# Second norm of a two-layer decoder: scale and shift as per-partition columns on the transposed blocks, on one Trainium2 core

## The chip, the cores and the metric

One core of a Trainium2 chip runs the whole program. The metric is the device time of one execution in microseconds (us), the median of several runs. The core has five engines with an instruction stream each: TensorE (PE, matrix products and transposes; its weight loads are shown apart as PEld), VectorE (DVE), ScalarE (ACT), GpSimdE (POOL) and SyncE (SP, which issues the DMAs). Each engine does its instructions in their order and waits on semaphores for the others.

## The reference

A token matrix x (1024 tokens, 1024 features, fp32) goes through two layers, each a mixer and a SwiGLU network. Each sub-layer normalises x, applies a shift and a scale that depend on a vector c, and adds its gated result to x:

```python
mod = (c_act @ ada_w[l] + ada_b[l])[:, None, :]
sh1, sc1, g1, sh2, sc2, g2 = jnp.split(mod, N_MOD, axis=-1)
...
x = x + g1 * (y @ w_out[l])
h = rms_norm(x, norm2_w[l]) * (1.0 + sc2) + sh2
gate, up = jnp.split(h @ w_gate_up[l], 2, axis=-1)
x = x + g2 * ((jax.nn.silu(gate) * up) @ w_down[l])
```

Here c_act is silu(c), and rms_norm(x, w) divides each token by the root of its mean square and multiplies feature by feature with w. The hidden width of the network is 2816. The change concerns the line that makes h: the scale (1 + sc2) times norm2_w, and the shift sh2, are 1024 numbers each, one a feature and the same for all tokens.

## The kernel before

**Tiles and precision.** The 1024 tokens lie as eight tiles X[t] of 128 tokens (partitions) by 1024 features. Products are done in fp32 accuracy by three matmuls of split operands (mm3, L134 to L136: high by high, high by low, low by high). A split (`split`) takes an ACT copy to the high half (L142) and a DVE subtraction for the low half (L139); hTh, hTl are the halves of the normalised input, gus those of the gate and up weights.

**Shift and scale.** The six modulation vectors of a layer come out of the products with ada_w as columns, mc, 128 partitions by 8 (feature 128 k + p stands in column k, partition p). ada_finish adds the bias (DVE, L380), for j = 4 forms (1 + sc2) times norm2_w (DVE, L383), turns the block on PE (L388, mcT), copies it from PSUM (ACT, L390, mr) and stores it to DRAM (L391). mod_row (L466) then reads a row back with a broadcast to all 128 partitions, 512 KB (L468, mrow). For the second norm that is j = 4 (scale) and j = 3 (shift), so that every partition holds the full row.

**The second norm.** norm2_a(t) calls rms_apply (L212): ACT squares the tile and sums along the row (L216, the square itself is thrown away into xn), POOL makes rs, the inverse root of the mean (ms and rs, L171 and L172), DVE computes x times rs times the scale row (L218, xn), and POOL adds the shift row (L220); for tile 3 DVE does this add. norm2_b(t) turns xn on PE, eight transposes of 128x128 (L478, hT, in two PSUM banks, kb = 0 and 1 for the lower and the upper four feature blocks), and ACT copies them out as hb, four copies of 128x256 a tile (L1386). In hb the features are on the partitions and the tokens along the row.

**The network.** Gate and up are computed by a Strassen-like scheme of seven products in the order b11, b21, t3, t2, t1, b22, t4. hb has four quarters: feature half kb by token half hf (hf 1 is tiles 4 to 7, hf 0 tiles 0 to 3). b11 and b21 are the two quarters of tiles 4 to 7, so they can start when those are normed; t3 and t2 are sums of quarters (build_t, whose additions are L1431, tile t), and t3, the first, needs quarters of tiles 0 to 3 too. That is why the norm's order is 4, 5, 6, 7, 0, 1, 2, 3: while the first products run, the last tiles are still normed, and behind tile 3 comes t3 = hb of tiles 0 to 3, upper features, less hb of tiles 0 to 3, lower features. The weights gur are loaded on SP's queue (L1439), combined on POOL (L1419) and split into gus. gu_pair adds products in the tiles p and u (p from gate by L1493 copies, L1498 additions from PSUM; silu on ACT, L1486, which has a table load ahead of it; the product, L1487; the store, L1488). The u copies are L1507 and L1512. Step functions run in an order given by strings of letters for each layer (O the output tile of the mixer, n and b the norm's two halves, h and t the splits); each also calls what it needs first. A scheduler then sets the order within each engine's stream from it, and pools of buffers (33 of 4 KB a partition in G, from which xn, hb and mrow are taken) limit what is under way. In the mixer's out_tile, DVE adds the group results oA, oB, oC of a tile to x (L1271) before the norm can take it.

Of the kernel before, what the change touches and what calls it, by code (L numbers as in the profile page):

```python
# [8 lines left out]
F32 = mybir.dt.float32  # L9
F32R = mybir.dt.float32r  # L10
I32 = mybir.dt.int32
AF = mybir.ActivationFunctionType
ALU = mybir.AluOpType
AX = mybir.AxisListType

P = 128
S = 1024
D = 1024
NT = S // P
KD = D // P  # L20
DEPTH = 2
# [25 lines left out]
R_N1, R_N2, R_AB, R_ON, R_BQ, R_BKV, R_BS, R_END = 0, 8, 16, 64, 72, 75, 77, 81  # L47
# [31 lines left out]
def tile_trunk(ctx, tc, x, c, positions, ada_w, ada_b, norm1_w, w_in, a_sinks, b_q_norm_w, b_w_uq,  # L79
# [3 lines left out]
    ACT, DVE, POOL, PE, DMA = nc.scalar, nc.vector, nc.gpsimd, nc.tensor, nc.sync  # L83

    cst = ctx.enter_context(tc.tile_pool(name="cst", bufs=1))
# [6 lines left out]
    def nm(s):  # L92
        uid[0] += 1
        return f"{s}_{uid[0]}"
# [13 lines left out]
    def G(shape, dt=F32, name="g"):  # L108
        return gp.tile(shape, dt, tag="g", name=nm(name), bufs=NG)
# [7 lines left out]
    def SM(shape, dt=F32, name="s"):  # L117
        return sp.tile(shape, dt, tag="s", name=nm(name))

    def TN(w=8, name="t"):  # L120
        t = tp.tile([P, 8], F32, tag="t", name=nm(name))
        return t[:, :w]

    def PA(name="pa"):
        return ps_pool["a"].tile([P, 512], F32, tag="a", name=nm(name))
# [43 lines left out]
    def rstd(dst, ss, n, w=1):  # L169
        v = TN(w, "ms")  # L170
        POOL.tensor_scalar(out=v, in0=ss, scalar1=1.0 / n, scalar2=EPS, op0=ALU.mult, op1=ALU.add)  # L171
        POOL.tensor_tensor(out=dst, in0=v, in1=mhalf[:, :w], op=ALU.pow)  # L172
# [39 lines left out]
    def rms_apply(xt, arow, shrow, eng=POOL):  # L212
        ss = TN(1, "ss")
        rs = TN(1, "rs")
        xn = G([P, D], F32, "xn")
        ACT.activation(out=xn, in_=xt, func=AF.Square, accum_out=ss)  # L216
        rstd(rs, ss, D)
        DVE.scalar_tensor_tensor(out=xn, in0=xt, scalar=rs, in1=arow, op0=ALU.mult, op1=ALU.mult)  # L218
        if shrow is not None:
            eng.tensor_tensor(out=xn, in0=xn, in1=shrow, op=ALU.add)  # L220
        return xn
# [76 lines left out]
    cols = []  # L298
# [66 lines left out]
    rows_done = set()  # L365
# [10 lines left out]
    cqd = [[dr.tile([P, 384], F32, name=f"cq{l}_{t}") for t in range(NT)] for l in range(DEPTH)]  # L376
    yad = [[dr.tile([P, 3, 512], F32, name=f"ya{l}_{hf}") for hf in range(2)] for l in range(DEPTH)]

    def ada_finish(l, j, mc, wait=1):
        DVE.tensor_tensor(out=mc, in0=mc, in1=cols[l][:, R_AB + 8 * j:R_AB + 8 * j + 8], op=ALU.add)  # L380
        if j in (1, 4):
            r = R_N1 if j == 1 else R_N2
            DVE.scalar_tensor_tensor(out=mc, in0=mc, scalar=1.0, in1=cols[l][:, r:r + 8],  # L383
                                     op0=ALU.add, op1=ALU.mult)
        for _ in range(wait):
            yield
        pt_ = PA("mcT")
        PE.transpose(pt_[:8, :P], mc, ident)  # L388
        mr = SM([P, 128], F32, "mr")
        ACT.copy(out=mr[:8, :], in_=pt_[:8, :P])  # L390
        DMA.dma_start(out=modd[l][j], in_=mr[:8, :])  # L391
        rows_done.add((l, j))
# [73 lines left out]
    def mod_row(l, j, alloc=G):  # L466
        t = alloc([P, D], F32, f"mrow{j}")
        DMA.dma_start(out=t, in_=modd[l][j].rearrange("r f -> (r f)").partition_broadcast(P))  # L468
        return t


    def transpose_tile(xn):

        r = []
        for kh in range(2):
            pv = PA("hT").rearrange("p (b f) -> p b f", f=P)
            for k in range(4):
                PE.transpose(pv[:, k, :], xn[:, (4 * kh + k) * P:(4 * kh + k + 1) * P], ident)  # L478
            r.append(pv)
        return r  # L480
# [66 lines left out]
    def layer(l, x_tiles):  # L547
# [32 lines left out]
        xns = {}  # L580
# [71 lines left out]
        if l == 0:  # L652
# [39 lines left out]
            def l_seq():  # L692
                for kp in range(4):
                    if kp >= 2:
                        need("a", 8)
                    raw_w.append(load_w1(kp, acc0[0]))
                    yield

            def s_seq():
                for kp in range(4):  # L700
                    need("l", kp + 1)
                    split_w1(raw_w[kp], POOL if SP0[kp] else DVE)
                    yield

            def h_seq():
                need("s", 2)
                for t in range(NE):
                    need("m", t + 1)
                    avq[t] = PA("avq")
                    in_proj(avq[t], T[t], w1, 0, 4)  # L710
                    yield

            def v_seq():
                need("s", 4)
                for t in range(NT):
                    if t < NE:
                        need("h", t + 1)
                    need("m", NE + t + 1 if t < NE else 2 * t + 2)
                    ps = avq[t] if t < NE else PA("avq")
                    in_proj(ps, T[t], w1, 4 if t < NE else 0)  # L720
                    avq_end(t, ps)
                    yield

            def c_seq():
                need("r", 2)
                consts.append(layer_consts(l, mod0[:, 4:5]))
                consts.append(setup_rest(mod0[:, 4:5]))
                run(consts[1])
                yield
                drain(consts[1])  # L730
                yield
# [5 lines left out]
            def bg_seq():  # L737
                need("C", 2)
                while run(bg):
                    yield  # L740

            def g_seq():
                need("r", 2)
                yield from g0
# [4 lines left out]
                                    l=l_seq(), s=s_seq(), h=h_seq(), v=v_seq(), C=c_seq(), G=g_seq(), B=bg_seq()))  # L749
# [483 lines left out]
        X = {}  # L1233
# [135 lines left out]
                yield  # L1369

        order = (4, 5, 6, 7, 0, 1, 2, 3)
        hb, hs, mods = {}, {}, []

        def norm2_a(t):
            xns[t] = rms_apply(X[t], mods[0], mods[1], DVE if t == 3 else POOL)
            DMA.dma_start(out=xm[l][t], in_=X[t])

        def norm2_b(t):
            hf, ts_ = t // 4, slice((t % 4) * P, (t % 4 + 1) * P)
            if t % 4 == 0:  # L1380
                for kb in range(2):
                    hb[kb, hf] = [(G if hf else W)([P, 2, 512], F32, "hb") for _ in range(2)]
            pvs = transpose_tile(xns.pop(t))
            for kb in range(2):
                for i in range(2):
                    ACT.copy(out=hb[kb, hf][i][:, :, ts_], in_=pvs[kb][:, 2 * i:2 * i + 2, :])  # L1386

# [232 lines left out]


        def mods_seq():
            mods.extend((mod_row(l, 4), mod_row(l, 3)))
            yield

        def norm_seq():
            need("k", 1)
            for n, t in enumerate(order):  # L1630
                need("O", 9 + n)
                norm2_a(t)
                yield

        def hb_seq():
            for n, t in enumerate(order):
                need("n", n + 1)
                norm2_b(t)
                yield
# [7 lines left out]
        def build_t_seq():  # L1647
            need("b", 8)
            need("h", 2)
            b11, b12, b21, b22 = hb[0, 1], hb[0, 0], hb[1, 1], hb[1, 0]  # L1650
            t2 = [G([P, 2, 512], F32, "t2") for _ in range(2)]
            tt2(t2, b22, b12, ALU.subtract)
            yield
            split_h("t3", t2)
            yield
            tt2(t2, t2, b11, ALU.add)
            split_h("t2", t2)
            yield
            tt2(b11, b12, b11, ALU.subtract)
            split_h("t1", b11)  # L1660
            yield
            split_h("b22", b22)
            yield
            tt2(b21, b21, t2, ALU.subtract)
            split_h("t4", b21)
            yield

        def load_gu_seq():
            gens[0] = gu_prep(load_gu(0))
            yield  # L1670

        def prep_gu_seq():
            need("j", 1)
            for n in range(2):
                ready.append(next(gens[0]))
                yield
# [12 lines left out]
        def pair_seq():  # L1689
            need("r", 2)  # L1690
            yield from pair_steps(0)

        seqs = dict(H=heads_seq(), S=soft_seq(), T=t_seq(), M=m_seq(), q=sq_seq(), a=ya_seq(), y=y_seq(), w=w_seq(),
                    g=g_seq(), x=x_seq(), O=o_seq(), k=mods_seq(), n=norm_seq(), b=hb_seq(), h=split_h_seq(),
                    t=build_t_seq(), j=load_gu_seq(), r=prep_gu_seq(), s=pair_seq())
        step, need = sequences(seqs)
# [34 lines left out]
        return X  # L1731

    X = layer(1, layer(0, None))
    fw = G([P, D], F32, "fw")
    DMA.dma_start(out=fw, in_=final_norm_w.partition_broadcast(P))
# [31 lines left out]
```

## Time and profile before

| what | value |
|---|---|
| median of the runs | 2379.6 us (2378.68 to 2386.13) |
| the profiled execution | 2386.33 us, of which 2384.6 us are the trace's span |
| mean granted clock of PE | 0.98 |
| DMA traffic | 349.78 MB, 147 GB/s over the span |
| stores to DRAM of modulation rows (L391) and broadcasts of them (L468) | 10 and 10 |
| shift additions on POOL / on DVE (L220) | 22 of 2.425 us mean / 2 of 1.22 us |
| copies hb (L1386) | 64 of 128x256, 0.388 us mean |

The profile is one execution. A row of a timeline has start, duration, engine, line, operation, the tiles written and read, and in brackets the time that the engine stood idle before it and what ended that idleness. A row of the waits has the waiting engine, tile and line, what it waited for, then the total, the number of times and the longest, in us. Of the 22 additions on POOL, 14 belong to the second norms and 8 to other norms; both on DVE belong to tile 3 of the second norms.

### The profile page before, as it was taken

The numbers are of one execution on the slowest core, as the hardware profiler recorded it, in microseconds if no ns is written. First come the engines' busy times: TensorE is split into PE (matmuls) and PEld (weight loads), VectorE is DVE, ScalarE is ACT, GpSimd is POOL, SyncE is SP. The second block draws the span as 40 slices with busy tenths as digits, with TensorE's granted clock in tenths as the row PEclk, the third lists the DMA queues.
The fourth block names the chain that finished last, engine by engine and source line by source line (L and its number), as shares of the span: only waits on it lengthen the run. The fifth ranks groups of instructions, "written<-read, shape, count | busy, mean of one in ns | idle before, by whom it ended". The sixth has DMA issues, their size and how long they took to land. (4 is left out here: it accounts for less than half of the span.)

```text
span 2384.6 us, 32002 instructions
## 1 busy us (share of the span) xinstructions
PE 2262.8 (95%) x11195; PEld 1907.2 (80%) x11195; DVE 1796.9 (75%) x2787; ACT 1099.1 (46%) x2244; POOL 1019.5 (43%) x1011
## 2 busy tenths in 40 slices
PE   5999899998999999999999899999989999999998
PEld 4789798887878787878878788988877888887786
DVE  7787578859768777699874875687698767648978
ACT  4566377625334343322344654784354444433233
POOL 4656630343323324455554655212435334225643
PEclk9999999999999999999999999999999999999999
DMA  7503432312566564872240154223125545467423
GB/s 254 165 19 113 170 131 89 112 48 93 168 208 233 178 235 167 307 274 89 80 162 22 55 178 142 80 80 115 54 84 188 192 154 181 164 219 288 155 106 115
DMA packets 156038, 349.78 MB, mean 147 GB/s; under 512 B 12619, under 2 KB 71781, under 8 KB 155877
## 3 DMA queue, kind: packets, MB, share of 16 engines
q1 hardware_dynamic: 155876, 347.74, 42.2%
q8 instruction: 88, 1.44, 0.2%
q14 instruction: 74, 0.60, 0.1%
HBM read 252.75 MB, written 94.94 MB: 146 GB/s over the span
## 5 line engine op out<-in xcount | busy, mean ns | idle before, releaser
L139 DVE TENSOR_TENSOR gus<-gur,gus 128x512 fp32r<-128x512 f32 x264 | 260.1, 1006 | 64.4 <-ACT gus L142 63.3
L142 ACT CAST gus<-gur 128x512 fp32r<-128x512 f32 x264 | 160.5, 621 | 223.9 <-PE gate L136 80.3
L134 PE MATMUL gate<-hTh,gus 128*128 128x512 f32 x616 | 243.3, 395 | 11.9 <-ACT u L1507 11.9
L134 PE MATMUL down<-dnt,dns 128*128 128x512 f32 x616 | 241.8, 393 | 11.6 <-issue 6.3
L135 PE MATMUL gate<-hTl,gus 128*128 128x512 f32 x616 | 241.8, 393 | 4.4 <-DVE hTl L139 4.4
L134 PE MATMUL up<-hTh,gus 128*128 128x512 f32 x616 | 241.8, 393 | 3.8 <-ACT u L1512 3.6
L135 PE MATMUL down<-dnt,dns 128*128 128x512 f32 x616 | 241.0, 391 | 1.3 <-DVE dnt L139 1.3
L136 PE MATMUL gate<-hTh,gus 128*128 128x512 f32 x616 | 241.5, 392 | 0.0
L135 PE MATMUL up<-hTl,gus 128*128 128x512 f32 x616 | 240.9, 391 | 0.0
L136 PE MATMUL down<-dnt,dns 128*128 128x512 f32 x616 | 240.9, 391 | 0.0
L136 PE MATMUL up<-hTh,gus 128*128 128x512 f32 x616 | 240.5, 390 | 0.0
L1419 POOL TENSOR_TENSOR gur<-gur 128x512 f32<-128x512 f32 x44 | 64.5, 1465 | 393.7 <-DVE gus L139 364.4
L142 ACT CAST dns<-act 128x512 fp32r<-128x512 f32 x132 | 81.8, 622 | 248.9 <-PE down L136 190.0
L1597 DVE TENSOR_TENSOR x<-x,down 128x512 f32<-128x512 f32 x224 | 147.9, 678 | 29.2 <-PE down L136 28.9
L139 DVE TENSOR_TENSOR dns<-act,dns 128x512 fp32r<-128x512 f32 x132 | 137.7, 1057 | 14.3 <-ACT dns L142 14.2
L134 PEld LDWEIGHTS gate<-hTh,gus 128*128 128x128 f32 x616 | 116.5, 189 | 39.6 <-ACT u L1507 14.9
L134 PEld LDWEIGHTS down<-dnt,dns 128*128 128x128 f32 x616 | 116.4, 189 | 39.1 <-issue 7.4
L135 PEld LDWEIGHTS gate<-hTl,gus 128*128 128x128 f32 x616 | 116.7, 189 | 29.7 <-DVE hTl L139 6.0
L134 PEld LDWEIGHTS up<-hTh,gus 128*128 128x128 f32 x616 | 116.6, 189 | 29.1 <-ACT u L1512 4.5
L135 PEld LDWEIGHTS down<-dnt,dns 128*128 128x128 f32 x616 | 116.4, 189 | 25.7 <-DVE dnt L139 1.7
L136 PEld LDWEIGHTS up<-hTh,gus 128*128 128x128 f32 x616 | 116.5, 189 | 24.6
L136 PEld LDWEIGHTS gate<-hTh,gus 128*128 128x128 f32 x616 | 116.5, 189 | 24.5
(410 smaller groups left out, 6158.8 us busy)
## 6 DMA issues: line engine op xcount, KB each, us to landing
gur<-in_w_gate_up_dram SPq DMA_DIRECT2D x88, 512.0 KB
ada<-in_ada_w_dram SPq DMA_DIRECT2D x80, 512.0 KB
wp<-wpe SPq DMA_DIRECT2D x77, 512.0 KB
dnt<-wp SPq DMA_DIRECT2D x77, 512.0 KB
dnr<-in_w_down_dram SPq DMA_DIRECT2D x44, 512.0 KB
act<-act SPq DMA_DIRECT2D x44, 512.0 KB
wr<-in_w_in_dram SPq DMA_DIRECT2D x24, 512.0 KB
act<-u SPq DMA_DIRECT2D x44, 256.0 KB
```

What stands on the lines that cost most here:

```text
L134: PE.matmul(ps, lh, rh, start=start, stop=False, skip_group_check=more)
L135: PE.matmul(ps, lh, rl, start=False, stop=False, skip_group_check=more)
L136: PE.matmul(ps, ll, rh, start=False, stop=stop, skip_group_check=more)
L139: eng.tensor_tensor(out=out_, in0=a, in1=b, op=ALU.subtract)
L142: ACT.copy(out=h, in_=src)
L1419: return lambda o, a, b, op: eng.tensor_tensor(out=o, in0=a, in1=b, op=op)
L1597: DVE.tensor_tensor(out=av_, in0=av_, in1=ps[t], op=ALU.add)
```

## The change

The columns of shift and scale stay where they are made. A constant tile modc[l], 128 by 16, holds the shift in columns 0 to 7 and the scale in columns 8 to 15, and ada_finish writes them there with the DVE steps that it had; for j = 3 and 4 it returns then, so the transpose, copy and store are gone, and so are the two broadcasts in mods_seq. norm2_a keeps the square and the inverse root; DVE multiplies x by rs alone (a tensor_scalar), and nothing is added. norm2_b applies scale and shift when it takes a transposed block out of PSUM: feature block k has its scale and shift in one column of modc, so ACT does eight activations a tile (Identity with a scale and a bias column, 128x128 each) instead of four copies. Four of tile 3, kb = 1, are DVE's (tensor_scalar, multiply and add).

```diff
+    modc = [cst.tile([P, 16], F32, name=f"modc{l}") for l in range(DEPTH)]
     def ada_finish(l, j, mc, wait=1):
-        DVE.tensor_tensor(out=mc, in0=mc, in1=cols[l][:, R_AB + 8 * j:R_AB + 8 * j + 8], op=ALU.add)
+        d = modc[l][:, 8 * (j == 4):8 * (j == 4) + 8] if j in (3, 4) else mc
+        DVE.tensor_tensor(out=d, in0=mc, in1=cols[l][:, R_AB + 8 * j:R_AB + 8 * j + 8], op=ALU.add)
         if j in (1, 4):
             r = R_N1 if j == 1 else R_N2
-            DVE.scalar_tensor_tensor(out=mc, in0=mc, scalar=1.0, in1=cols[l][:, r:r + 8],
+            DVE.scalar_tensor_tensor(out=d, in0=d, scalar=1.0, in1=cols[l][:, r:r + 8],
                                      op0=ALU.add, op1=ALU.mult)
+        if j in (3, 4):
+            rows_done.add((l, j))
+            return
...
         def norm2_a(t):
-            xns[t] = rms_apply(X[t], mods[0], mods[1], DVE if t == 3 else POOL)
+            ss = TN(1, "ss")
+            rs = TN(1, "rs")
+            xn = xns[t] = G([P, D], F32, "xn")
+            ACT.activation(out=xn, in_=X[t], func=AF.Square, accum_out=ss)
+            rstd(rs, ss, D)
+            DVE.tensor_scalar(out=xn, in0=X[t], scalar1=rs, scalar2=None, op0=ALU.mult)
...
         def norm2_b(t):
...
-            pvs = transpose_tile(xns.pop(t))
-            for kb in range(2):
-                for i in range(2):
-                    ACT.copy(out=hb[kb, hf][i][:, :, ts_], in_=pvs[kb][:, 2 * i:2 * i + 2, :])
+            for kb, pv in enumerate(transpose_tile(xns.pop(t))):
+                for i in range(4):
+                    d, k = hb[kb, hf][i // 2][:, i % 2, ts_], 4 * kb + i
+                    a, b = modc[l][:, 8 + k:9 + k], modc[l][:, k:k + 1]
+                    if t == 3 and kb == 1:
+                        DVE.tensor_scalar(out=d, in0=pv[:, i, :], scalar1=a, scalar2=b, op0=ALU.mult, op1=ALU.add)
+                    else:
+                        ACT.activation(out=d, in_=pv[:, i, :], func=AF.Identity, scale=a, bias=b)
...
         def mods_seq():
-            mods.extend((mod_row(l, 4), mod_row(l, 3)))
+            assert {(l, 3), (l, 4)} <= rows_done
```

The change also moves instructions, alike in both layers. Names carry a number for each buffer; line numbers in the new kernel are 16 higher behind the norm. The next rows are DVE's stream in layer 1 from the scaling of tile 3 (xn) to the low half of the first t3 operand (hTl), as it was:

```order
L218 SCALAR_TENSOR_TENSOR xn_16942<-x_16441,rs_16941,mrow_3257_16407 128x1024
L139 TENSOR_TENSOR gus_17051<-gur_16665,gus_17051 128x512
L220 TENSOR_TENSOR xn_16942<-xn_16942,mrow_3258_16409 128x1024
L1498 TENSOR_TENSOR p_3344_16829<-p_3344_16829,gate_16888 128x512
L139 TENSOR_TENSOR gus_17054<-gur_16669,gus_17054 128x512
L139 TENSOR_TENSOR gus_17059<-gur_16667,gus_17059 128x512
L1431 TENSOR_TENSOR t_3366_16964<-hb_16799,hb_16797 128x1024
L1431 TENSOR_TENSOR t_3367_16965<-hb_16800,hb_16798 128x1024
L1498 TENSOR_TENSOR p_3344_16829<-p_3344_16829,up_16889 128x512
L1487 TENSOR_TENSOR p_3344_16829<-p_3344_16829 128x512
L139 TENSOR_TENSOR hTl_16969<-t_3366_16964,hTh_16968 128x1024
```

And as it is in the changed kernel:

```order
L1386 TENSOR_SCALAR xn_16961<-x_16439,rs_16960 128x1024
L139 TENSOR_TENSOR gus_17073<-gur_16667,gus_17073 128x512
L139 TENSOR_TENSOR gus_17076<-gur_16671,gus_17076 128x512
L1514 TENSOR_TENSOR p_3332_16841<-p_3332_16841,gate_16900 128x512
L139 TENSOR_TENSOR gus_17081<-gur_16669,gus_17081 128x512
L1400 TENSOR_SCALAR hb_16807<-hT_16973,modc_357 128x128 x2
L1400 TENSOR_SCALAR hb_16808<-hT_16973,modc_357 128x128 x2
L1514 TENSOR_TENSOR p_3332_16841<-p_3332_16841,up_16901 128x512
L1447 TENSOR_TENSOR t_3354_16986<-hb_16807,hb_16805 128x1024
L1447 TENSOR_TENSOR t_3355_16987<-hb_16808,hb_16806 128x1024
L1503 TENSOR_TENSOR p_3332_16841<-p_3332_16841 128x512
L139 TENSOR_TENSOR hTl_16991<-t_3354_16986,hTh_16990 128x1024
```

The shift's addition is gone, four evictions (hb) have come, and the addition of the up product to p, which needs PE's last matmul of it, stands ahead of the two t steps instead of behind them.

POOL's stream in layer 1 from tile 1's to tile 3's inverse root, before:

```order
L171 TENSOR_SCALAR ms_16791<-ss_16787 128x1
L172 TENSOR_TENSOR rs_16788<-ms_16791,mhalf 128x1
L220 TENSOR_TENSOR xn_16789<-xn_16789,mrow_3258_16409 128x1024
L1419 TENSOR_TENSOR gur_16667<-gur_16667,s_3313_16731 128x4x128
L171 TENSOR_SCALAR ms_16906<-ss_16902 128x1
L172 TENSOR_TENSOR rs_16903<-ms_16906,mhalf 128x1
L220 TENSOR_TENSOR xn_16904<-xn_16904,mrow_3258_16409 128x1024
L1419 TENSOR_TENSOR gur_16671<-gur_16671,s_3314_16732 128x4x128
L171 TENSOR_SCALAR ms_16944<-ss_16940 128x1
L172 TENSOR_TENSOR rs_16941<-ms_16944,mhalf 128x1
```

And now:

```order
L171 TENSOR_SCALAR ms_16800<-ss_16796 128x1
L172 TENSOR_TENSOR rs_16797<-ms_16800,mhalf 128x1
L1435 TENSOR_TENSOR gur_16669<-gur_16669,s_3301_16741 128x4x128
L1435 TENSOR_TENSOR gur_16673<-gur_16673,s_3302_16742 128x4x128
L171 TENSOR_SCALAR ms_16918<-ss_16914 128x1
L172 TENSOR_TENSOR rs_16915<-ms_16918,mhalf 128x1
L171 TENSOR_SCALAR ms_16963<-ss_16959 128x1
L172 TENSOR_TENSOR rs_16960<-ms_16963,mhalf 128x1
```

The additions are gone, and both weight combinations (gur) now stand ahead of the inverse root of tile 2 (the second ms and rs), where one stood ahead and one behind.

More of the change, by code (lines that the diff above doesn't have):

```diff
@@ L1371, in layer @@
         order = (4, 5, 6, 7, 0, 1, 2, 3)
-        hb, hs, mods = {}, {}, []
+        hb, hs = {}, {}
         def norm2_a(t):
-            xns[t] = rms_apply(X[t], mods[0], mods[1], DVE if t == 3 else POOL)
+            ss = TN(1, "ss")
[4 more added lines that the diff above has]
+            DVE.tensor_scalar(out=xn, in0=X[t], scalar1=rs, scalar2=None, op0=ALU.mult)
             DMA.dma_start(out=xm[l][t], in_=X[t])
```

## The prediction

> **What bounds the kernel now.** I read the engine totals first, then TensorE's waits, then the timelines round the longest of those that the change can reach.
>
> ```profile
> PE 2262.8 (95%) x11195; PEld 1907.2 (80%) x11195; DVE 1796.9 (75%) x2787; ACT 1099.1 (46%) x2244; POOL 1019.5 (43%) x1011
> ...
> PE gate L134 <- ACT u L1507: 11.9, 6, 2.8
> PE hT L478 <- DVE xn L220: 9.9, 2, 5.0
> PE hT L478 <- POOL xn L220: 6.5, 3, 4.1
> ...
> PE gate L135 <- DVE hTl L139: 4.4, 2, 2.2
> ```
>
> PE is busy 95% of the span, so an edit to other engines pays only where PE stands still. It stands still for the second norm in three rows (total, times, longest): twice 5.0 us, once a layer, for the shift added to token tile 3 (L220, on DVE); for POOL's adds (1.2 us in each second norm; the third, 4.1, is a first norm, untouched); twice 2.2 us for the first low half made behind it (hTl). That is some 8.4 us a layer. PE there, in layer 1 (start, duration, idle before and releaser), the same place in layer 0 (555.13), and layer 1's stretch with its granted clock, 0.77:
>
> ```profile
> 1710.94 1.09 PE L478 MATMUL hT<-ident,xn 128*128 128x128 f32 x8 [1.23 <-POOL xn L220]
> ...
> 1738.72 1.97 PE L478 MATMUL hT<-ident,xn 128*128 128x128 f32 x8 [4.95 <-DVE xn L220]
> ...
> 1741.34 0.63 PE L136 MATMUL up<-hTh,gus 128*128 128x512 f32 x1
> 1741.77 0.63 PE L134 MATMUL up<-hTh,gus 128*128 128x512 f32 x1
> ...
> 1744.49 0.39 PE L136 MATMUL up<-hTh,gus 128*128 128x512 f32 x1
> 1744.72 0.40 PE L134 MATMUL gate<-hTh,gus 128*128 128x512 f32 x1
> ...
> 1747.59 0.50 PE L135 MATMUL gate<-hTl,gus 128*128 128x512 f32 x1 [2.24 <-DVE hTl L139]
> ...
> 555.13 1.97 PE L478 MATMUL hT<-ident,xn 128*128 128x128 f32 x8 [4.95 <-DVE xn L220]
> ...
> 1730.00:1745.00 15.00, 10.05 (x47) 8.42 (x46) 12.47 (x15) 9.02 (x21) 4.73 (x4) 0.77 0.31 105
> ```
>
> Behind the 4.95 us stall the matmuls take 0.63 instead of 0.39 us (a step of 0.43, where 1744.49 to 1744.72 has 0.23). Eight transposes and twelve matmuls last from 1738.72 to 1744.88, 6.2 us; at full clock about 0.85 for the transposes (1.09 with its overlap, 1710.94) and 12 x 0.23 = 2.8, 3.6 in all. So the stall costs some 2.5 us more. Layer 0 stalls as long, at 555.13.
>
> **The change part by part.** I follow layer 1; DVE first.
>
> ```profile
> 1720.52 4.18 DVE L139 TENSOR_TENSOR hTl<-hb,hTh 128x1024 fp32r<-128x1024 f32 x2
> ...
> 1727.61 1.29 DVE L218 SCALAR_TENSOR_TENSOR xn<-x,rs,mrow 128x1024 f32<-128x1024 f32 x1 [1.65 <-POOL rs L172]
> 1728.81 0.69 DVE L139 TENSOR_TENSOR gus<-gur,gus 128x512 fp32r<-128x512 f32 x1
> ...
> 1730.08 2.23 DVE L139 TENSOR_TENSOR gus<-gur,gus 128x512 fp32r<-128x512 f32 x1
> 1732.23 0.74 DVE L1271 SCALAR_TENSOR_TENSOR x<-oB,rsb,x 128x512 f32<-128x512 f32 x1
> ...
> 1735.64 1.28 DVE L218 SCALAR_TENSOR_TENSOR xn<-x,rs,mrow 128x1024 f32<-128x1024 f32 x1 [0.44 <-POOL rs L172]
> ...
> 1737.44 1.22 DVE L220 TENSOR_TENSOR xn<-xn,mrow 128x1024 f32<-128x1024 f32 x1
> ...
> 1741.13 2.36 DVE L1431 TENSOR_TENSOR t<-hb,hb 128x1024 f32<-128x1024 f32 x2 [0.67 <-ACT hb L1386]
> ...
> 1744.91 0.69 DVE L1498 TENSOR_TENSOR p<-p,up 128x512 f32<-128x512 f32 x1 [1.42 <-PE up L136]
> ...
> 1746.32 2.35 DVE L139 TENSOR_TENSOR hTl<-t,hTh 128x1024 fp32r<-128x1024 f32 x2
> ```
> ```profile
> 1720.08 2.40 POOL L220 TENSOR_TENSOR xn<-xn,mrow 128x1024 f32<-128x1024 f32 x1 [1.59 <-DVE xn L218]
> 1725.38 1.28 POOL L1419 TENSOR_TENSOR gur<-gur,s 128x512 f32<-128x512 f32 x1 [2.90 <-DVE gus L139]
> ...
> 1729.04 2.72 POOL L220 TENSOR_TENSOR xn<-xn,mrow 128x1024 f32<-128x1024 f32 x1 [1.47 <-DVE xn L218]
> ...
> 1734.73 0.88 POOL L172 TENSOR_TENSOR rs<-ms,mhalf 128x1 f32<-128x1 f32 x1
> ```
> ```profile
> 1733.00 1.06 ACT L216 ACTIVATE xn<-x 128x1024 f32<-128x1024 f32 x1 [5.42 <-DVE x L1271]
> ...
> 1735.56 2.28 ACT L1386 COPY hb<-hT 128x256 f32<-128x256 f32 x8
> ...
> 1741.39 1.28 ACT L1486 ACT_TABLE_LOAD   x1
> 1742.68 0.63 ACT L1486 ACTIVATE p<-p 128x512 f32<-128x512 f32 x1
> 1743.22 1.03 ACT L142 CAST hTh<-t 128x1024 fp32r<-128x1024 f32 x1
> ```
>
> *POOL's adds go.* While one runs, DVE is slow beside it: the hTl pair takes 4.18 us under the add of 1720.08 and 2.35 without one; a gus takes 2.23 under the add of 1729.04 and 0.69 without. That is 1.83 and 1.54 us.
>
> *The scaling loses its second tensor.* The xn step (1.28) becomes x times rs. The trace has an operation of DVE with one tensor source of this size:
>
> ```profile
> L254 DVE TENSOR_SCALAR acc<-ada,cact x10: 735/746/1847, 94.3 to 1403.7; 128x1024 f32<-128x1024 f32 x10
> 264.93 0.37 ACT L834 ACTIVATE QK<-ukv,rskv 128x128 f32<-128x128 f32 x1 [0.53 <-PE ukv L136]
> 265.20 0.46 ACT L836 ACTIVATE QK<-ukv,rskv 128x256 f32<-128x256 f32 x1
> ```
>
> I take its median, 0.75, so 0.5 us less each time.
>
> *Up to tile 3's sum.* rs of tile 2 now stands behind both of POOL's gur steps (one moves ahead, 1.28). They start at 1725.38 − 1.83 = 1723.55, end at 1726.1, and rs follows at 1726.9; xn ends at 1727.65 instead of 1728.8. One gus has moved ahead of it, so oA's sum (0.75), a gus (0.69) and oB's sum (0.74) end at 1729.8, where now it is 1732.97: 3.2 us earlier. Bounds: 0, if POOL's rs comes as late as DVE saves, and 4.4, if rs has no wait at all (1.65 less, short of what the moved gus takes).
>
> *Tile 3.* From the square's start to xn's it is 1735.64 − 1733.00 = 2.64; so xn runs from 1732.4 to 1733.2, and the shift's 1.22 us with the gus ahead of it is gone (1738.7 now). PE, rid of tile 7's wait of 1.23, is free for tile 3 at 1738.72 − 4.95 − 1.23 = 1732.5: a stall of 0.7 instead of 4.95, and up ends 3.6 us later, at 1736.8 instead of 1744.9.
>
> *ACT is next in line.* Eight and four copies of 128x256 before the table load become sixteen and four activations of 128x128, each with a scale and a bias column. They begin where the copies began, shifted by the square: 1735.56 − 3.2 = 1732.4. Their price isn't in the trace. The nearest rows: an activation of 128x128 from PSUM with one column takes 0.37 and lets the next one start after 0.27; copies step 2.28/8 = 0.285. The upper end is 0.46, the full duration of the row of twice the size. I take 0.36, about the full duration of the one-column row, nearest to it in size and operands. Then 20 x 0.36 = 7.2 us, to 1739.6; at 0.27, 1.8 us sooner; at 0.46, 2.0 later.
>
> The Trainium skill, page "ScalarE: Activation LUTs", section "What ACT_TABLE_LOAD costs", gives an activation 186 ns + 0.833 ns an element, about 93 ns more for each column operand and about 93 ns of overlap with the next. For the one-column row that is 386 ns, near the 0.37 here; for two columns it would be a step of 0.386, 20 of them 7.7 us, and the sum 1.0 us worse over both layers.
>
> *Then DVE.* The two t (1.18 each) run 1739.6 to 1742.0; the product p (0.69) waits for the table (1.28) and silu, 1741.5, so it ends at 1742.7. The cast on ACT ends at 1742.5. From hTl's start to PE's it is 1747.59 − 1746.32 = 1.27: PE resumes at 1744.0, **3.6 us earlier**. The add p<-p,up, moved ahead of t, costs nothing: up is done at 1736.8, 3 us before t can start. The four evictions that DVE takes (one-tensor operations) lie beside ACT's.
>
> *What comes back.* PE now idles from 1736.8 to 1744.0, more than 4.95, so the slow clock comes after it: 2.5 us over the next products. Behind them PE waits again, for a chain that starts with DVE behind this tile and goes through POOL and a load, so it moves up by the 3.6:
>
> ```profile
> 1765.23 1.82 DVE gus L139 x3
> ...
> 1799.14 0.50 PE L134 MATMUL gate<-hTh,gus 128*128 128x512 f32 x1 [2.52 <-ACT u L1507]
> ...
> 613.73 0.50 PE L134 MATMUL gate<-hTh,gus 128*128 128x512 f32 x1 [1.09 <-ACT u L1507]
> ...
> 327.93 0.27 PE L388 MATMUL mcT<-ident,mc 128*8 128x128 f32 x1 [1.24 <-DVE mc L380]
> ```
>
> The 2.52 cover the 2.5 in layer 1. In layer 0 the same wait is 1.09 (613.73), and 1.4 us are lost.
>
> *At nothing.* Per layer two mcT transposes, two small copies and stores, and two broadcasts of a row to 512 KB leave. The only one of the removed transposes that PE waited for cost 1.24 us (327.93, for DVE mc); other work of PE may take its place: 0, bounds 0 to 1.2 in all. The broadcasts land long before they are used: 0, bounds 0 to 1.0. They leave SP's queue; a gur load in layer 1 goes ahead of a store and three loads, inside the DMA time of the chain above: 0.
>
> *Sum.* 2 x 3.6 − 1.4 = 5.8 us. The profiled execution is 2386.3 (its span 2384.6), 6.7 over the median of 2379.6; both lose as much: 2380.5, and **2373.8 for the median**. About 0.3%, 7.1 us (2372.5 to 2386.7 counts as the same), is what can be told from no change.
>
> **The rivals.**
> *Cheap evictions.* ACT steps 0.27 as behind the one-column row, so 1.8 a layer more: 5.4 x 2 − 1.4 = 9.4, 2370.2; with 4.4 upstream instead of 3.2, 2367.8. For it: copies step 0.285. Against it: a second column.
> *The slow clock decides.* If PE has no wait left behind the gap that takes the slow clock in, 2.5 is lost in both layers: 2 x (3.6 − 2.5) = 2.2, 2377.4. For it: 0.63 us matmuls after 4.95 us of idleness, and the gap here is 7.2; and the wait of 2.52 ends with a load, not with DVE. The Trainium skill, page "TensorE: Matmul & The Clock Gate", section "What's actually happening", has half rate after an idle window of about 3.4 us until one such window is busy; the 0.77 agrees. By it the gap makes PE slow in both layers for some 3.4 us, a loss of about 1.7 each, an estimate; this rival would then give 2 x 1.9, 2375.8.
> *Dear evictions.* At 0.46, 2.0 a layer less: 1.6 x 2 − 1.4 = 1.8, 2377.8; with half of the 3.2 upstream, 2381.0.
> *Slower: the add ahead of t.* p<-p,up waits for PE's up matmuls, and now the two t and all behind them on DVE queue behind it. If tile 3's xn comes no earlier than now, up ends at 1744.9 as now; then 0.7 + 2.36 + 0.69 and the 1.27 give 1749.9, 2.3 a layer later, and a second slow clock (2.5) may follow: 2 x 2.3 to 2 x 4.8, 2384 to 2389, 2386 likeliest. It costs from where tile 3's transposes start behind 1736.4 (6.2 to up's end and 5.0 behind it make 1747.6). For it: a wait of DVE on PE in the row of 1744.91. Against it: 3.2 us upstream, and the shift's 1.22.
>
> **How the numbers follow.** Forecast 0.44 (its own range 2370.5 to 2377; faster 0.18, same 0.26). Cheap evictions 0.20, faster. Slow clock 0.14, same. Dear evictions 0.10, same. Add ahead of t 0.12 (slower 0.10, same 0.02). So faster 0.38, same 0.52, slower 0.10. The range goes from 2367 (cheap, with early upstream, and 0.8 of the removed waits) to 2381 (dear, late upstream); outside are the slower rival and a little.
>
> **What would show it.** Right: the wait hT <- DVE xn falls to under 1.5 us in each layer; no 2 us gus round tile 2's norm; activations of hb at a step near 0.36; a PE gap of 6 to 8 us before the first t3 product with matmuls of 0.63 behind it. Wrong: a step of 0.27 or 0.46; t waiting for p<-p,up; a hT wait that stays near 5; hTl pairs that remain above 4 us (then DVE was not slowed by POOL).

## The result, and the profile after

The changed kernel takes 2371.5 us (median of 14 runs, 2367.0 to 2378.6) where the kernel before takes 2385.3 (14 runs, 2378.7 to 2389.3): ratio 0.9948, 95% interval 0.9940 to 0.9957. By the ratio that is 12.4 us less, by the medians 13.8, where the prediction had 5.8. The forecast of 2373.8 lies close, and the range holds the time, but the closeness is luck: the forecast started from the first three runs of before, whose median of 2379.6 turned out 5.7 us low, and that hid most of a gain that was put too small. Measured as a difference, the gain is twice the forecast.

The engine totals and TensorE's waits of the changed kernel (total, times, longest; its line numbers are 6 to 16 higher):

```profile
PE 2258.4 (95%) x11191; PEld 1904.2 (80%) x11191; DVE 1775.4 (75%) x2793; ACT 1120.9 (47%) x2296; POOL 984.8 (42%) x997
...
PE gate L134 <- ACT hTh L142: 8.1, 2, 4.1
PE gate L134 <- ACT u L1523: 6.9, 6, 1.8
...
PE hT L484 <- POOL xn L220: 4.1, 1, 4.1
...
PE hT L484 <- DVE p L1514: 2.3, 2, 1.1
...
PE hT L484 <- DVE xn L1386: 0.4, 2, 0.2
```

The two stalls of 4.95 us for tile 3 are 0.2 us each, tile 7's 1.2 us are gone, and so are the 2.2 us for hTl. In their place PE waits 4.1 us a layer for the first cast of t3 (hTh), and 1.1 us for DVE's addition p<-p,gate, which frees the PSUM bank of tile 3's second half. That wait stood nowhere in before: there the transposes began so late (1738.72) that this addition ended (1739.26) while the first half was being turned.

The same place in layer 1 on PE, DVE and ACT. All of it lies 11.2 us earlier than in before already when the stretch begins:

```profile
1721.26 0.66 PE L484 MATMUL hT<-ident,xn 128*128 128x128 f32 x4 [0.21 <-DVE xn L1386]
1723.06 0.66 PE L484 MATMUL hT<-ident,xn 128*128 128x128 f32 x4 [1.14 <-DVE p L1514]
...
1730.54 0.79 PE L134 MATMUL gate<-hTh,gus 128*128 128x512 f32 x1 [4.05 <-ACT hTh L142]
...
1731.80 0.79 PE L135 MATMUL gate<-hTl,gus 128*128 128x512 f32 x1
1732.39 0.63 PE L136 MATMUL gate<-hTh,gus 128*128 128x512 f32 x1
```
```profile
1709.49 1.23 DVE L139 TENSOR_TENSOR hTl<-hb,hTh 128x1024 fp32r<-128x1024 f32 x1 [1.06 <-ACT hTh L142]
...
1715.26 0.75 DVE L1386 TENSOR_SCALAR xn<-x,rs 128x1024 f32<-128x1024 f32 x1 [2.68 <-POOL rs L172]
...
1716.59 0.68 DVE L139 TENSOR_TENSOR gus<-gur,gus 128x512 fp32r<-128x512 f32 x1
1717.19 0.74 DVE L1277 SCALAR_TENSOR_TENSOR x<-oB,rsb,x 128x512 f32<-128x512 f32 x1
...
1726.53 0.69 DVE L1514 TENSOR_TENSOR p<-p,up 128x512 f32<-128x512 f32 x1 [1.41 <-PE up L136]
1727.13 2.35 DVE L1447 TENSOR_TENSOR t<-hb,hb 128x1024 f32<-128x1024 f32 x2
```
```profile
1720.53 7.08 ACT L1402 ACTIVATE hb<-hT,modc 128x128 f32<-128x128 f32 x20
1727.63 1.28 ACT L1502 ACT_TABLE_LOAD   x1
```

The hTl step takes 1.23 and the gus 0.68 us, where before had 4.18 for a pair and 2.23. The twenty activations take 7.08 us, a step of 0.354. Then the slow clock (0.63 us matmuls, the granted clock at half) comes behind the gap.

To see where the 15.8 us between the two profiled spans (2384.6, 2368.8) arise, each PE matmul of one trace is set beside the same matmul of the other. The table gives the time from one place of the program to the next in us, the places named by before's time there, for every kernel of this study, one profile each:

| kernel | to 300 | 300–345 | 515–650 (norm 0) | 650–960 | 960–1690 | 1690–1815 (norm 1) | 1815–2375 |
|---|---|---|---|---|---|---|---|
| before | 300.0 | 45.0 | 135.0 | 310.0 | 730.0 | 125.0 | 560.0 |
| before, again | 301.5 | 45.0 | 135.4 | 306.8 | 734.5 | 123.7 | 563.3 |
| changed | 299.3 | 44.1 | 131.7 | 304.5 | 729.2 | 120.3 | 560.1 |
| changed, again | 299.4 | 44.1 | 131.4 | 302.8 | 730.9 | 119.7 | 558.8 |
| rows_back | 298.4 | 45.0 | 131.3 | 308.7 | 732.1 | 119.7 | 560.7 |
| rows_off | 301.8 | 44.1 | 134.9 | 308.2 | 729.1 | 124.6 | 561.2 |
| pool_add | 298.8 | 44.1 | 137.1 | 312.1 | 732.3 | 123.7 | 562.0 |
| pool_beside | 299.6 | 44.1 | 134.8 | 305.8 | 731.8 | 122.9 | 559.1 |
| plain_copies | 302.1 | 44.1 | 128.3 | 304.9 | 728.7 | 116.0 | 559.4 |
| dve_none | 300.0 | 44.1 | 133.0 | 307.3 | 733.0 | 121.4 | 558.9 |
| dve_more | 300.9 | 44.1 | 131.7 | 306.6 | 730.1 | 120.2 | 558.9 |
| late_silu | 299.5 | 44.1 | 131.1 | 308.4 | 732.6 | 120.6 | 560.3 |
| late_more | 301.7 | 44.1 | 134.4 | 310.1 | 730.8 | 121.8 | 560.2 |

From 345 to 515 us every kernel takes 170.0, to within 0.1. Means of two profiles each: layer 0's norm stage gains 3.6 us, layer 1's 4.4, the place of the removed column transposes 0.9, and the stage with the weight waits of layer 0 (650 to 960) 4.8, where before's own two profiles are 3.2 apart. The other columns differ by as much between two runs of one kernel as between the two kernels. The profile of pool_add is the slowest of its twelve runs, that of plain_copies the fastest of its six, so their columns lean that way.

### The profile page after: what moved, and what is told of

Read it like the earlier page. It is cut to its first block, busy times and chain, and to the rows that moved or that the text cites. A ratio compares the mean times of both kernels' runs of the same rounds, so it can differ in the third digit from the quotient of the medians.

```text
span 2368.8 us, 31988 instructions
## 1 busy us (share of the span) xinstructions
PE 2258.4 (95%) x11191; PEld 1904.2 (80%) x11191; DVE 1775.4 (75%) x2793; ACT 1120.9 (47%) x2296; POOL 984.8 (42%) x997
## 5 line engine op out<-in xcount | busy, mean ns | idle before, releaser
L139 DVE TENSOR_TENSOR gus<-gur,gus 128x512 fp32r<-128x512 f32 x264 | 248.3, 961 | 60.3 <-ACT gus L142 59.5
L134 PEld LDWEIGHTS down<-dnt,dns 128*128 128x128 f32 x616 | 116.2, 189 | 38.5 <-issue 6.8
L134 PEld LDWEIGHTS up<-hTh,gus 128*128 128x128 f32 x616 | 116.1, 189 | 28.7 <-ACT u L1528 4.9
L135 PEld LDWEIGHTS down<-dnt,dns 128*128 128x128 f32 x616 | 116.5, 189 | 25.8 <-DVE dnt L139 1.7
L136 PEld LDWEIGHTS down<-dnt,dns 128*128 128x128 f32 x616 | 116.5, 189 | 24.5
```

The source lines that it names most:

```text
L134: PE.matmul(ps, lh, rh, start=start, stop=False, skip_group_check=more)
L135: PE.matmul(ps, lh, rl, start=False, stop=False, skip_group_check=more)
L136: PE.matmul(ps, ll, rh, start=False, stop=stop, skip_group_check=more)
L139: eng.tensor_tensor(out=out_, in0=a, in1=b, op=ALU.subtract)
```

## The experiments

Each ratio is to the kernel before, run beside it, with its 95% interval; a cut in the code is marked by three dots.

**The changed kernel again**, unedited. 

> The changed kernel once more, for a second profile and as the anchor of this chip. Ratio to the kernel before 0.994 to 0.9957 (some 12 us less). Theory A (8 us come from the two norm stages, 1 us from the removed transposes, and the rest from weight waits in layer 0 that happen to end with or without a slow clock): the first two parts stand in this profile again within 0.5 us, the rest does not have the same places or sizes. Rival B (removed rows and their DMA bring the rest everywhere): the rest stands at the same places, with the same sizes.

Measured 0.9947 (0.9932 to 0.9962). Norm stages and the 0.9 us are there again within 0.6 us. Of the rest, 650 to 960 us is low in both profiles (304.5, 302.8), but not by the same waits: the one at 692.9 us of before lasts 1.23 and 1.83 us, the one at 938.9 us 1.79 and 1.13.

**Before again**, unedited, one profile. 

> The kernel before once more, for a second profile. Theory A: the stalls of both second norms (1.2, 4.95 and 2.2 us) are there within 0.1 us, and the weight waits of layer 0 between 600 and 950 us have other sizes, by some us in all. Rival: every wait is the same as in the first profile.

The stalls of 1.2 and 4.95 us return to the tenth. Of the two for hTl, layer 1's is 0.5 us shorter: the clock was at half for 3.4 us there, in the first profile for 6.8.

```profile
PE gate L134 <- ACT u L1507: 11.5, 7, 2.7
PE hT L478 <- DVE xn L220: 9.9, 2, 5.0
...
PE gate L135 <- DVE hTl L139: 3.8, 2, 2.1
```

But 650 to 960 us is 306.8 instead of 310.0. The row behind the difference is the last large weight wait of layer 0, first in before, then in the changed kernel:

```profile
938.86 0.79 PE L134 MATMUL gate<-hTh,gus 128*128 128x512 f32 x1 [2.80 <-ACT u L1507]
```
```profile
931.24 0.50 PE L134 MATMUL gate<-hTh,gus 128*128 128x512 f32 x1 [1.79 <-ACT u L1523]
```

Behind 2.80 us the clock is slow (0.79, the length of the slow rows above); behind 1.79 it isn't. Set beside the matmuls ahead of it, those 10 us behind it come 3.8 us earlier in the changed kernel: 1.0 for the wait, 2.8 for the clock. The length of the wait alone doesn't decide it: in this second profile of before the same wait lasts 2.66 us, the clock stays full, and those 10 us come 2.8 us earlier. How the wait lies against the clock's own steps does, as the last section shows.

**pool_add: POOL's additions back**, on a row of zeros, for the seven tiles that had them; the order of all other engines is the same.

```diff
             DVE.tensor_scalar(out=xn, in0=X[t], scalar1=rs, scalar2=None, op0=ALU.mult)
+            if t != 3:
+                POOL.tensor_tensor(out=xn, in0=xn, in1=zrow[0], op=ALU.add)
...
```

> The changed kernel with POOL's addition of 128x1024 put back for seven tiles a layer (a row of zeros is added); every other engine's order is the same. Theory A: DVE is slowed beside POOL again (hTl pair near 4 us instead of 2.36, a gus of 2 us), tile 7's transposes wait 1 us for POOL again, tile 2 comes 3 us later, and 2 to 3 us a layer come back: ratio about 0.997. Rival C (the slow hTl and gus had another cause, and only DVE's shorter steps count): hTl stays near 2.4, and under 1 us a layer comes back, 0.9955 at most.

Measured 0.9999 (0.9985 to 1.0013): the whole gain is given back, more than either theory had. So the rest of the change taken together (a scaling with one tensor, no addition for tile 3, activations for copies) gains nothing that shows while POOL adds. Its POOL and DVE in layer 1:

```profile
1722.77 2.40 POOL L1388 TENSOR_TENSOR xn<-xn,zrow 128x1024 f32<-128x1024 f32 x1 [0.87 <-DVE xn L1386]
...
1732.78 2.40 POOL L1388 TENSOR_TENSOR xn<-xn,zrow 128x1024 f32<-128x1024 f32 x1 [0.87 <-DVE xn L1386]
```
```profile
1712.45 0.75 DVE L1277 SCALAR_TENSOR_TENSOR x<-oB,rsb,x 128x512 f32<-128x512 f32 x1
...
1723.27 4.12 DVE L139 TENSOR_TENSOR hTl<-hb,hTh 128x1024 fp32r<-128x1024 f32 x2
...
1733.28 2.45 DVE L139 TENSOR_TENSOR gus<-gur,gus 128x512 fp32r<-128x512 f32 x1
...
1746.56 0.69 DVE L1516 TENSOR_TENSOR p<-p,up 128x512 f32<-128x512 f32 x1 [2.60 <-PE up L136]
```

POOL's second addition ends at 1735.18, and the gus that began at 1733.28 ends at 1735.73, 0.55 us behind it; the hTl pair ends 2.2 us behind the first addition's end (1725.17), about the two steps' own time (2.36 where no addition of POOL runs, at 1718.86). So DVE did not run slower, it stood still until POOL's instruction was over. The sum x<-oB, whose second tensor lies in PSUM, took its usual 0.75 at 1712.45 beside another of POOL's additions. The Trainium skill, page "SBUF — State Buffer", section "SBUF: two separate sides", says so: the port pair that DVE and GpSimd share is an exclusive lock, held for the whole instruction, which a DVE operation with two SBUF inputs also needs. These rows agree.

**pool_beside: the same, without the chain.** POOL adds as long at the same places, into a spare tile that nobody waits for.

```diff
-                POOL.tensor_tensor(out=xn, in0=xn, in1=zrow[0], op=ALU.add)
+                POOL.tensor_tensor(out=zrow[1], in0=xn, in1=zrow[0], op=ALU.add)
```

> As with POOL's addition put back, but its result goes to a spare tile: POOL works as long, at the same places, and no transpose waits for it. Contention (DVE is slow beside POOL's addition, and tile 3 comes late for that): hTl pair near 4.1 and a gus of 2.4 us as with the addition put back, tile 3's transposes wait 2.6 us again, ratio to the kernel before 0.998 to 1.000. Latency (tiles come late because xn passes through one engine more): as the changed kernel, 0.994 to 0.996.

Measured 0.9982 (0.9970 to 0.9994): two thirds of the gain are gone though no tile passes through POOL. Tile 3 comes late as with the addition on the path:

```profile
1714.52 4.12 DVE L139 TENSOR_TENSOR hTl<-hb,hTh 128x1024 fp32r<-128x1024 f32 x2
...
1724.53 2.45 DVE L139 TENSOR_TENSOR gus<-gur,gus 128x512 fp32r<-128x512 f32 x1
```
```profile
PE hT L484 <- DVE xn L1386: 5.2, 2, 2.6
```

Of the 9.3 us that pool_add loses in the two norm stages against the changed kernel, pool_beside loses 6.2, by one profile each. Contention is the larger part; the way through POOL the smaller.

**rows_back and rows_off: the rows' path alone.** The first puts transposes, copies, stores and broadcasts back beside the changed kernel, unused (POOL reads eight columns of each row behind tile 3, which holds the buffers until then). The second takes them out of the kernel before and fills its two rows on POOL with 1 and 0, so that scale and shift are left out.

```diff
-        if j in (3, 4):
-            rows_done.add((l, j))
-            return
...
+            dead.extend((mod_row(l, 4), mod_row(l, 3)))
```
```diff
...
-            mods.extend((mod_row(l, 4), mod_row(l, 3)))
+            mods.extend((G([P, D], F32, "mrow4"), G([P, D], F32, "mrow3")))
+            for r, v in zip(mods, (1.0, 0.0)):
+                POOL.memset(r, v)
```

> The changed kernel with the rows' path put back beside it, its result unused: two transposes, two small copies, two stores and two broadcasts of 512 KB a layer, and the two buffers held until behind tile 3. Theory A: 0.9 us of a transposed column's wait come back and little else, ratio 0.995. Rival B: half of the 12 us come back, ratio 0.997 to 0.998.

> The kernel before without the rows' path alone: no transpose, copy, store and broadcast for the second norm; its rows are two tiles that POOL fills with 1 and 0, so scale and shift are left out, and the norm keeps its steps, POOL's additions too. If the rows' path is worth what the profiles show (0.9 us where PE waited for the column in layer 0, 1 to 1.5 us at 1440 to 1520 us in layer 1): ratio to the kernel before 0.9985 to 0.9995. If it is worth what putting it back cost (some 5 us): 0.9975 to 0.9985.

Measured 0.9966 (0.9953 to 0.9979) and 0.9999 (0.9985 to 1.0013). Putting the rows back cost about 4.5 us, with an interval that overlaps that of the changed kernel; taking them out alone gained nothing that shows. Both profiles agree on one place, the 0.9 us at 300 to 345: rows_off has them, and in rows_back PE waits as in before:

```profile
326.36 0.27 PE L391 MATMUL mcT<-ident,modc 128*8 128x128 f32 x1 [1.24 <-DVE modc L383]
```

Most of what else rows_back loses is in 650 to 960 us (308.7, and 308.2 in rows_off), where the two are alike though one has the path and the other not. So the rows are worth 0.9 us for sure, and no more was shown.

**plain_copies: cheap evictions.** ACT copies 128x256 blocks; scale and shift are left out.

```diff
-                for i in range(4):
...
-                        ACT.activation(out=d, in_=pv[:, i, :], func=AF.Identity, scale=a, bias=b)
+                for i in range(2):
+                    ACT.copy(out=hb[kb, hf][i][:, :, ts_], in_=pv[:, 2 * i:2 * i + 2, :])
```

> The changed kernel with plain ACT copies of 128x256 in place of the activations, all sixteen of tiles 1 to 3 on ACT; scale and shift are left out. Theory A (ACT's evictions set when t3 starts): ACT needs 12 x 0.285 = 3.4 us instead of 7.1 ahead of the table load, PE's gap shrinks by 2 to 3 us a layer and the slow clock behind it goes: 6 to 10 us less than the changed kernel, ratio 0.9905 to 0.9925. Rival D (something else, DVE's queue or the weights, sets it): 0 to 2 us less, ratio 0.994 to 0.995.

```profile
1719.15 3.40 ACT L1397 COPY hb<-hT 128x256 f32<-128x256 f32 x12
1722.57 1.28 ACT L1497 ACT_TABLE_LOAD   x1
```
```profile
PE gate L134 <- ACT hTh L142: 3.2, 2, 1.6
...
PE gate L135 <- DVE hTl L139: 2.1, 2, 1.0
```

ACT's 7.1 us become 3.4, the gap 1.6, and the norm stages are 3.3 and 4.0 us shorter, with half clock gone in layer 1 and down from 6.8 to 3.4 us in layer 0. So ACT's queue did set t3's start. Yet the time is 0.9937 (0.9923 to 0.9952), between the two forecasts and only 2.4 us less than the changed kernel, and the intervals overlap. In its profile the gain of the norm stages isn't lost behind them: against the mean of the changed kernel's two profiles 2.8 us are lost before 300 us, ahead of anything that was edited, and 1.3 from 650 to 960. How much of the 7 us lasts, these runs don't show.

**dve_none and dve_more: who evicts.** All on ACT (24 ahead of the table load), or tile 2's upper four on DVE too (16).

```diff
-                    if t == 3 and kb == 1:
+                    if False:
```
```diff
-                    if t == 3 and kb == 1:
+                    if t in (2, 3) and kb == 1:
```

> The changed kernel with all evictions on ACT, 24 ahead of the table load. If ACT's queue sets t3's start: 4 x 0.354 = 1.4 us later a layer, ratio 0.9955 to 0.9965. If DVE's share (four steps of 0.34) delayed the t as much: no change, 0.9945 to 0.995.

> The changed kernel with tile 2's four upper blocks evicted by DVE too: ACT has 16 activations ahead of the table load instead of 20, and the addition of up to p stands behind the two t again. If ACT's queue sets t3's start: 1.4 us earlier a layer (PE from 515 to 580 and 1690 to 1765 us), and with SP's and the weights' order as in the changed kernel it is kept: ratio 0.993 to 0.994. If DVE, which sets the weights' loads behind, is later for it: the gain is back by the weight waits at 605 to 650 and 1765 to 1815, ratio 0.9945 to 0.996.

Measured 0.9973 (0.9961 to 0.9986) and 0.9961 (0.9947 to 0.9975). Without DVE's help ACT takes 8.51 us, and PE waits 5.5 us instead of 4.05:

```profile
1729.15 8.51 ACT L1402 ACTIVATE hb<-hT,modc 128x128 f32<-128x128 f32 x24
```
```profile
PE gate L134 <- ACT hTh L142: 11.0, 2, 5.5
```

That is the forecast 1.4 us a layer, and the norm stages are longer by as much (133.0, 121.4). The time is 6 us above the changed kernel's, twice what that explains and outside the forecast; in the profile, which is 9.6 us longer than the changed kernel's two in the mean, 6.6 lie from 650 to 1690, in stages that vary. With more help the wait falls to 2.7, but PE then waits 0.6 to 0.9 for hTl, the norm stages are as long as in the changed kernel, and the interval overlaps with that kernel's. The slow clock came in all the same.

**late_silu and late_more: the table load behind the casts.** The first silu is queued behind the second t3 cast, alone or with dve_more's evictions.

```diff
-            finish(p1[:, 0, :], p1[:, 1, :], 0, 0)
+            if j == 0:
+                while "t3" not in casts:
+                    step("t")
+                with tc.issue_after(casts["t3"].ins):
+                    finish(p1[:, 0, :], p1[:, 1, :], 0, 0)
...
```

> The changed kernel with the first silu and its table load issued behind the two casts that the first t3 product needs. If ACT's queue sets when t3 starts: the table's 1.28 and silu's 0.54 leave the path, t (on DVE) comes next, PE's gap shrinks from 4.05 to about 2.9 us, 1.1 us a layer, and if 2.9 is too short for the slow clock, 2 us a layer more: 2 to 6 us less than the changed kernel, ratio 0.9925 to 0.994. If the weight waits behind it give everything back: 0.9945 to 0.9955.

> The same, and tile 2's four upper blocks evicted by DVE too, which takes 4 x 0.354 = 1.4 us from ACT and 1.4 to DVE; the addition of up to p stands behind the two t again. If both ACT's evictions and the wait of p for up hold t3: the gap falls below 2 us, the slow clock goes in both layers, 4 to 9 us less than the changed kernel, ratio 0.991 to 0.993. If the weight waits behind it give it back: 0.9945 or more.

Measured 0.9963 (0.9948 to 0.9977) and 0.9976 (0.9963 to 0.9990): no gain, and with late_more a loss. The gap shrank to 3.0 and 2.0 us, as expected. What failed lies behind it. In late_silu PE, back 1.1 us sooner in layer 0, then waits 0.57 us for hTl, and the slow clock ends only 0.2 us sooner (last section); the norm stages, 131.1 and 120.6 us, are the changed kernel's. In late_more PE is ahead of the changed kernel, counted from the start of the stage, by 0.5 to 0.8 us in layer 0 and 2.2 in layer 1 until the next weight wait. There it loses that and more: the wait lasts 2.36 and 2.76 us, where the changed kernel has at most 0.33 and 0.61, and half clock follows it. In late_more's layer 0:

```profile
612.48 0.80 PE L134 MATMUL gate<-hTh,gus 128*128 128x512 f32 x1 [2.36 <-ACT u L1530]
```

The loads for those weights start later. SP's waits (520 to 600 us) and its issues in layer 0, first of the changed kernel, then of late_silu, then of late_more:

```profile
SPq L1455 <- DVE gus L139: 26.1, 5, 18.5
...
556.27 0.34 SPq L1504 DMA_DIRECT2D act<-p  x1
575.23 2.10 SPq L1455 DMA_DIRECT2D gur<-in_w_gate_up_dram  x2
```
```profile
SPq L1505 <- DVE p L1504: 25.8, 1, 25.8
```
```profile
574.92 0.34 SPq L1505 DMA_DIRECT2D act<-p  x1
576.78 0.97 SPq L1456 DMA_DIRECT2D gur<-in_w_gate_up_dram  x2
```
```profile
575.50 0.34 SPq L1505 DMA_DIRECT2D act<-p  x1
580.08 0.97 SPq L1456 DMA_DIRECT2D gur<-in_w_gate_up_dram  x2
```

With silu late, the store of p waits 25.8 us at the head of SP's queue, but that by itself holds up little: in the changed kernel the load waits as well, 18.5 us, for DVE's gus steps, which free the weight buffers. Those steps moved: the first is at 574.39 in the changed kernel and comes behind p's product in late_silu (575.95) and behind more hTl steps in late_more (578.64). Counted from the matmul at 515 us of before, the first load starts 1.3 us later in late_silu and 2.4 in late_more, and in late_more layer 0's stage is 3 us longer than in the changed kernel (134.4), although its t3 began sooner. That the late loads make the longer wait fits the order of the chain; no run changed the loads alone.

## Why the prediction was right or wrong

**Bound and stages: right.** PE's stalls in the norm stage went as said, and ACT's evictions became what sets t3 (plain_copies, dve_none). One sign failed: the gap ahead of t3 was to be 6 to 8 us and is 4.05. The prediction counted it to the first product with hTl, but two with hTh come first, and up ended 0.9 us later than it had.

**Contention with POOL's additions: right, and larger than thought.** The prediction took the hTl and gus rows as slowed beside POOL; pool_beside shows that this alone is 6.2 of the 9.3 us. It named the two places, but not the mechanism.

**Upstream, 3.2 us: measured 3.8.** (The numbers are layer 1's; before's scale is the changed kernel's time plus 11.2 us.) The last sum of tile 3 ends at 1717.93, 1729.1 on before's scale, where 1729.8 was forecast. xn takes 0.75 as said. DVE, early now, waits 2.68 us for POOL's rs behind both gur steps; that wait sets tile 2, as the sum had it. Its upper bound of 4.4 does not follow from its rows: without any wait for rs the four savings, 1.83, 1.54, 0.5 and 1.65, make 5.5.

**Evictions, 0.36: measured 0.354.** The estimate of 0.386 from the Trainium skill, page "ScalarE: Activation LUTs", section "What ACT_TABLE_LOAD costs", was dearer than the measured one. They begin at 1731.7 on before's scale (1732.4 forecast). PE resumes with hTl at 1743.0 there, not 1744.0: **4.6 us earlier instead of 3.6** (3.9 in layer 0).

**The add ahead of t: harmless, but narrowly.** The prediction gave it 3 us of room. PE's up matmuls end at 1726.5, 0.9 us later on before's scale than forecast, because of the wait for the PSUM bank; p<-p,up ends at 1727.2, and ACT's evictions at 1727.6. The room was 0.4 us. In pool_add it is used up: there p waits 2.60 us for up, until 1746.56, and the t behind it.

**The slow clock: right in kind, and smaller than thought.** It came in both layers, but from the first product with hTl on it took back 1.2 to 1.8 us, not 2.5. The weight wait behind it took most of that in: in layer 1 it fell from 2.52 to 0.61 and 0.06 in the two profiles, and 4.4 us are left at 1815 in their mean. In layer 0 it fell from 1.09 to 0.33 and 0.20, and 3.6 us are left. So the norm stages gained 8.0 us, where 2 x 3.6 − 1.4 = 5.8 was forecast.

**"At nothing" was wrong for the column:** the wait of 1.24 us was bounded at 0 to 1.2 and taken at 0; it brought 0.9.

**What the sum did not have** is the stage of layer 0's weight waits, 650 to 960 us. There the changed kernel is 4.8 us shorter in the mean of two profiles; over all kernels the stage takes 302.8 to 312.1 us. Two things move it: how long PE waits there, and how long the clock is at half. Before's two profiles (310.0 and 306.8) wait alike, 11.9 and 12.1 us, but are at half clock for 10.2 and 3.4 us. The changed kernel's (304.5 and 302.8) wait 9.8 and 10.1 us, at half clock for 3.4 us and not at all. So about 2 of the 4.8 us are shorter waits, and most of the rest is the clock, which two runs of one kernel do not have alike. Why the waits are shorter stays open: rows_back has the changed kernel's norm stages and waits 12.3 us. The norm stages and the column explain 8.9 of the 12.4 us; the other 3.5 rest on this stage, or on places that vary as much from run to run.

What failed is therefore the size of the sum, not its path: its norm stages were 2.2 us too small (PE's return was put 0.3 to 1.0 us a layer too late, the slow clock's price too high), the column 0.9, and about 3.5 us come from outside the places that it counted.

## What to carry to other kernels

Before moving work off an engine, look at what its instructions hold up elsewhere: one row of another engine that takes three times its usual length beside them is a term of the sum, at each place where the two overlap. A gain of PE in front of a chain of loads can be lost at the next wait for them, if the engine that frees their buffers doesn't gain as well (late_more); so follow the first load behind the place, not only the first matmul. And whether a wait of 2 to 3 us brings half clock with it depends on how it happens to lie against the clock's steps, which differs from run to run: profile the same kernel twice before such a stage is put into a sum.

## What the runs showed of the hardware

- A DVE subtraction of two SBUF tensors that begins inside a POOL addition of 128x1024 ends about its own time after POOL's end: 2.45 us instead of 0.68 for 128x512, 4.12 instead of 2.36 for two of 128x1024. A DVE step with one tensor in PSUM was not held up (0.75 us at 1712.45 of pool_add).
- The granted clock moves in steps. In the clock records of all thirteen profiles it is full or half, and every change lies on a grid of 3.413 us that runs through the whole execution and lies against the program in one way in one run and in another in the next. These are two such steps each of before and of before again, round the wait at 938.86 that lasted 2.80 and 2.66 us; a row has the stretch, its length, the busy time of PE, PEld, DVE, ACT and POOL, the granted clock, and the DMA's share and GB/s:

```profile
934.69:938.11 3.42, 1.37 (x7) 0.79 (x5) 1.37 (x3) 1.55 (x3) 2.67 (x2) 1.00 0.96 360
938.11:941.52 3.41, 2.66 (x6) 2.15 (x7) 2.07 (x2) 1.70 (x4) 3.33 (x3) 0.50 0.01 2
```
```profile
936.08:939.49 3.41, 1.56 (x7) 0.94 (x5) 1.29 (x2) 1.49 (x3) 2.72 (x2) 1.00 0.89 330
939.49:942.90 3.41, 2.61 (x11) 2.18 (x12) 3.11 (x2) 1.76 (x4) 3.33 (x4) 1.00 0.01 6
```

  PE was busy for 0.40 of the first step in the one and 0.46 in the other. Over all profiles, half clock followed each of the 179 full-clock steps with PE busy for under 0.42 of the time, 37 of the 88 from there to 0.54, and none of the 8308 above; full clock came back only behind a step with PE busy for 0.81 or more. So what counts is how much of a wait falls into one step. (The shares are rough, as the ends of matmuls are modelled.)
- So a slow stretch need not end sooner when PE restarts sooner. In layer 0 of the changed kernel PE resumes at 556.51 behind 4.09 us, in late_silu at 555.64 behind 2.99, and the last slow matmuls are these, of the one and of the other (half clock is granted from 555.07 to 561.90, and from 555.10 to 561.92; the two profiles are within 0.3 us of each other at this point of the program):

```profile
561.35 0.63 PE L134 MATMUL gate<-hTh,gus 128*128 128x512 f32 x1
```
```profile
561.44 0.62 PE L135 MATMUL gate<-hTl,gus 128*128 128x512 f32 x1
```

  The restart that came 0.9 us sooner bought slow matmuls.
- An ACT activation of 128x128 from PSUM with a scale and a bias column steps at 0.354 us, a copy of 128x256 at 0.283.
